# A one-core Hymba layer: the output stage's buffers moved, its mixing in place, the sample attention over another stage's memory, and other steps for the plan

## The chip, the cores and the metric

The kernel runs on one core of a Trainium2 chip. Its engines are TensorE (PE in the profile, with its weight loads as PEld), VectorE (DVE), ScalarE (ACT), GpSimd (POOL) and SyncE (SP, which here issues all the DMAs). Each engine takes its own instructions strictly in the order in which they stand; they wait for one another through semaphores. The metric is the time of one execution in microseconds of the device, as the median of the runs.

## The reference

One step of a one-layer hybrid decoder, on a prompt of 2048 tokens and a sample of 8 sequences with 8 tokens each, with model width 1024. Cut to what is computed:

```python
h = rmsnorm(x, norm_w)
q, k, v, qb, kb, vb, low, ga, gb = split(h @ w_in)          # one input projection
# mixer A: 8 heads x 64, q and k normed and rotated
branches = [dilated_attention(q, k, v, w, d) for w, d in ((128, 1), (512, 4), (2048, 16))]
oA = sum(softmax(lse of the branches)[g] * branches[g] for g in range(3))
# mixer B: gated linear attention (GLA), 4 heads, key 64, value 128
S[t] = exp(log_a[t]) * S[t-1] + kb[t] outer vb[t];  oB[t] = rmsnorm(qb[t] @ S[t])
y = x + concat(oA * silu(ga), oB * silu(gb)) @ w_out
```

The sample's queries see a cache of 2048 earlier keys and values for each sequence and an initial GLA state. Outputs are `y` for prompt and sample, the window of keys and values, the GLA states, and the sample's new keys and values.

## The kernel before, in words

**Tiles and stages.** The 2048 prompt tokens are 16 tiles of 128 rows; the sample's 64 rows are one more tile, called s. The stages overlap:

- Input stage. `prep` norms a tile of x, cuts it into two f16 parts and turns it with PE; `prep_first` does tiles s and 0 first, whose transposes are called th (early parts `early_ht`, result `hl`). `fetch_w` and `load_w` fetch the weight blocks v, k, q, qkb (GLA's q and k), g, vb, gb and at the end o0 and o1, the two halves of w_out. `fetch_w` reads a block, takes its maximum (mx_v on PE spreads it over the partitions), makes a scale `ns_v`, and cuts the block into an f16 high part on ACT (L1278) and a low part on DVE (L1279). `project` (L1728) multiplies a block with all 17 tiles, block after block, in accumulators acc_v, acc_k and so on (L1748). The tiles come back from DRAM as `hr`.
- Attention of the prompt (`unit`, `branch3`, `attend`): scores s, exponentials p, transposes t of p, products O with v. These are woven between the projections of q, qkb and g. The three branches are written to DRAM (`o_d`) with 66 numbers per head: 64 values, a denominator and a maximum.
- GLA (`gla_prompt`): chunks of 128 rows, worked in pairs e0 to e7. For a chunk there are scores (sc_e), a decay matrix `full` copied by ACT (L891), the product O with the old state `Sbd`, U (the new keys times the values, L1906), and four updates of the state on DVE (L1927). A norm follows (`gla_out`), and the chunk goes to DRAM as `ob_d`.
- Gates. `silu` (L1294) takes the accumulators of g and gb and writes ga and gw; `so_g` and `so_gb` are its tiles.
- Output stage. `scales` turns the maxima so far into the factors `smx` and `smxa` by which a tile's mixture is scaled into f16 range. `combine(t)` (L2124) loads the three branches of tile t as oc and GLA's result and the gates as ob, gw, ga, and mixes them into mix; `parts_of` (L2063) cuts mix into an f16 high and low part (mt); `turned` (L2070) transposes both (tm on PE, mh behind it); `finish` (L2097) does 48 matmuls Y (L2111) with w_out and adds x, which is loaded again as xr.
- Sample attention (`sample_pair`, `values`) for pairs of sequences: keys from the cache, scores, and products OS with the value tiles sv_b (four blocks of 512 columns, 1 MB) and sv_w (one block). It is woven between the Y of the output stage.

**What sets the order.** `weave` runs such generators in turn, and so writes the whole program down. Then the class `Plan` reads what was written: which instruction needs which, which tile lies in whose memory (a gate that opens only when the former holder is done), and a price for each instruction. `settle` works through the program backward and forward several times and so gives every instruction a priority; it then adds some hand-found numbers to the priorities of some of them, deals a last order, and `fix` ties every engine to it:

```python
prio = [-f for f in self.rank()]
for _ in range(rounds):
    self.order(prio, bias)
    prio = [-x for x in self.backward(self.start)]
...
plan.fix(plan.settle(7, 600.0, 1.15, 60.0, 10.0, steps))
```

`steps` was a list of seeds; `moved` (L637) drew from each which instruction is meant, how far the number reaches (its tile, itself, or neighbours in time on its engine), and the number. `land` (600) is added to the landing time of each DMA. So when one tile changes its memory, or one number changes, the order may change on all five engines, anywhere in the program.

**Memory.** Pools lie on the left or the right of each partition's memory. Pools of the input stage are wr (four slots for weight blocks), zp (two of each tag), hp (four, tag hl) and hps (one). They lie on the right and close at the end of the projection of gb. GLA's pools lie on the left. When GLA is done they close, and the output pools cb and cb1 take that memory: oc, mix, ob, gw, ga, mt, mh, xr and the small w, dw, mn, with two slots each, and three product tiles tc (tags t0 to t2) with one. The sample attention (sk2 and ss1) takes the input stage's memory on the right. `first_mixes` (L2197) mixes tiles 0 and 1 ahead of the output stage, beginning after gb's tile 11, and turns tile 0 after tile 14; it stands woven with the projection of gb and the loads of w_out.

## Time and profile before

| | |
|---|---|
| time, median of 3 runs | 1262.98 us (1262.38 to 1268.51) |
| the profiled execution | 1262.71 us, of which the profile's span is 1260.9 us |
| DVE, ACT, POOL busy | 956.1, 817.8, 549.0 us |
| mean traffic of the DMA queues | 225 GB/s, 283.08 MB |
| last projection (gb) ends | 1008.1 us after the span's start |
| output stage | 1008 to 1261 us |

The profile is one execution on the chip. A row of the list of waits gives the engine, the tile and line that waited, what released it, and then the total in us, the count and the longest. A row of the timeline gives the start, the duration, the engine, line, operation and tiles, the count of equal instructions that it stands for, and in brackets the idle time just ahead of it with its releaser. A row of grouped instructions gives `out<-in`, shape and count, then busy time and mean ns of one, then idle time ahead. The rows of slices divide the span by 40; a digit is the busy share in tenths, and PEclk is the granted clock of PE in tenths. The row by windows gives a stretch, its length, and then for each engine busy time and count, with the granted clock, the DMA share and GB/s at the end.

### The profile page before, as it was taken

The numbers are of one execution on the slowest core, as the hardware profiler recorded it, in microseconds if no ns is written. First come the engines' busy times: TensorE is split into PE (matmuls) and PEld (weight loads), VectorE is DVE, ScalarE is ACT, GpSimd is POOL, SyncE is SP. The second block draws the span as 40 slices with busy tenths as digits, with TensorE's granted clock in tenths as the row PEclk, the third lists the DMA queues.
The fourth block names the chain that finished last, engine by engine and source line by source line (L and its number), as shares of the span: only waits on it lengthen the run. The fifth ranks groups of instructions, "written<-read, shape, count | busy, mean of one in ns | idle before, by whom it ended". The sixth has DMA issues, their size and how long they took to land.

```text
span 1260.9 us, 26211 instructions
## 1 busy us (share of the span) xinstructions
PE 1202.4 (95%) x8942; PEld 723.7 (57%) x8942; DVE 956.1 (76%) x2450; ACT 817.8 (65%) x2191; POOL 549.0 (44%) x475
## 2 busy tenths in 40 slices
PE   5999999999999999998999999999999969999998
PEld 2444465667566566766677656665666435445443
DVE  7987887999889777777877557788888795269562
ACT  6654697889599888968778424678878632123220
POOL 0155433665755244643444766646533162024230
PEclk9999999999999999999999999999999979999999
DMA  8579935876945898699997867564435689988842
GB/s 291 187 213 270 258 126 138 233 200 188 231 153 148 232 251 301 183 272 273 265 272 231 242 184 195 172 209 137 139 135 193 217 299 343 381 333 326 323 169 68
DMA packets 235832, 283.08 MB, mean 225 GB/s; under 512 B 116193, under 2 KB 146866, under 8 KB 232626
## 3 DMA queue, kind: packets, MB, share of 16 engines
q1 hardware_dynamic: 235698, 281.40, 73.7%
q8 instruction: 71, 1.16, 0.4%
q14 instruction: 63, 0.52, 0.1%
HBM read 183.02 MB, written 75.24 MB: 205 GB/s over the span
## 4 chain that ended last, share of the span: by engine, by line
PE 53%; ACT 15%; DVE 15%; DMA 8%; issue 6%; SPq 2%; POOL 2%; DVEq 0%; ACTq 0%; POOLq 0%
PE Y L2111 13%; PE acc_v L1748 5%; PE acc_qkb L1748 4%; PE acc_k L1748 4%; PE acc_q L1748 3%; PE acc_vb L1748 3%; PE t L1046 3%; ACT p L1039 3%; PE O L1061 3%; PE s L1028 3%; PE acc_g L1748 3%; DMA o_d<-o 2%; PE OS L2360 2%; DMA qb<-q_d 2%; DVE p L1036 2%
## 5 line engine op out<-in xcount | busy, mean ns | idle before, releaser
L1748 PEld LDWEIGHTS <-hr 128*128 128x128 f16 x1824 | 172.0, 98 | 112.8 <-issue 13.2
L1603 POOL TENSOR_TENSOR pr<-k,qb 128x512 f32<-128x512 f32 x128 | 168.2, 1314 | 148.2 <-DVE sck L1604 73.9
L1039 ACT ACTIVATE p<-p,o 128x256 f32<-128x256 f32 (+1 forms) x384 | 173.7, 458 | 24.7 <-DVE o L1036 24.2
L1748 PEld LDWEIGHTS <-hl 128*128 128x128 f16 x1248 | 120.0, 98 | 119.5 <-issue 5.6
L2111 PE MATMUL Y<-w_o,mh 128*128 128x512 f16 x768 | 178.5, 383 | 2.4 <-ACT mh L2077 1.3
L1013 POOL TENSOR_TENSOR pt<-p,pt 128x512 f16<-128x512 f32 (+1 forms) x80 | 91.4, 1142 | 147.2 <-ACT pt L1012 124.1
L1061 PE MATMUL O<-v,pt 128*128 128x128 f16 x1200 | 135.6, 219 | 5.4 <-DVE pt L1009 1.9
L1046 PE MATMUL t<-ident,p 128*128 128x128 f32 x600 | 123.5, 278 | 4.7 <-ACT p L1039 3.0
L2111 PEld LDWEIGHTS <-mh 128*128 128x128 f16 x768 | 73.5, 99 | 89.5 <-issue 7.7
L1604 DVE TENSOR_REDUCE sck<-pr 128x8 f32<-128x512 f32 x128 | 86.9, 679 | 45.6 <-POOL pr L1603 45.2
L1061 PEld LDWEIGHTS <-pt 128*128 128x128 f16 x1200 | 93.7, 98 | 37.9 <-DVE pt L1009 4.6
L1748 PE MATMUL acc_g<-w_g,hr 128*128 128x256 f16 (+1 forms) x768 | 112.0, 276 | 0.0
L1748 PE MATMUL acc_v<-w_v,hl 128*128 128x512 f16 x384 | 108.5, 383 | 0.4 <-ACT zs_q L1323 0.4
L1748 PE MATMUL acc_k<-w_k,hl 128*128 128x512 f16 x384 | 104.4, 379 | 0.5 <-DVE vp L1410 0.4
L1748 PE MATMUL acc_vb<-w_vb,hr 128*128 128x512 f16 x384 | 100.9, 379 | 3.9 <-DVE so_g L1297 3.4
L1748 PE MATMUL acc_q<-w_q,hl 128*128 128x512 f16 x384 | 102.4, 379 | 0.1
L2159 POOL TENSOR_TENSOR tc<-oc,w 128x512 f32<-128x512 f32 x32 | 43.9, 1390 | 125.1 <-DVE w L2151 97.7
L1036 DVE CUSTOM_DVE_ANT_0 p<-s,m3w,scl_s 128x128 f32<-128x128 f32 (+1 forms) x256 | 87.7, 394 | 12.1 <-PE s L1028 4.7
L1748 PE MATMUL acc_gb<-w_gb,hr 128*128 128x512 f16 x384 | 94.8, 380 | 0.0
L1028 PE MATMUL s<-kk,qq 128*128 128x256 f16 (+1 forms) x512 | 87.7, 264 | 4.8 <-DVE o L1036 2.9
L1046 PEld LDWEIGHTS t<-ident,p 128*128 128x128 f32 x600 | 74.6, 141 | 26.8 <-ACT p L1039 11.5
L1748 PE MATMUL acc_qkb<-w_qkb,hr 128*128 128x512 f16 x288 | 81.0, 379 | 0.0
(528 smaller groups left out, 2532.4 us busy)
## 6 DMA issues: line engine op xcount, KB each, us to landing
k<-in_cache_k_win SPq DMA_DIRECT2D x104, 256.0 KB
sv_b<-in_cache_v_win SPq DMA_DIRECT2D x24, 1024.0 KB
hr<-h_d SPq DMA_DIRECT2D x44, 512.0 KB
qb<-q_d SPq DMA_DIRECT2D x64, 256.0 KB
oc<-o_d SPq DMA_DIRECT2D x48, 264.0 KB
o_d<-o SPq DMA_DIRECT2D x64, 132.0 KB
x<-in_x_prompt SPq DMA_DIRECT2D x16, 512.0 KB
h_d<-hl SPq DMA_DIRECT2D x16, 512.0 KB
```

The lines of the kernel that those rows point to most:

```text
L1013: POOL.tensor_tensor(l, f, h, ALU.subtract)
L1028: PE.matmul(s_ps[:, i * w : (i + 1) * w], q, k, start=(n == 0), stop=(n == len(prods) - 1),)
L1036: DVE.tensor_tensor_reduce(s[:, sl], s_ps[:, sl], mask, neg, BIG, ALU.add, ALU.min, nmf(i))
L1039: ACT.activation(s[:, sl], s[:, sl], AF.Exp, bias=nmf(i), scale=-1.0, accum_out=denf(i))
L1046: PE.transpose(p_ps[:, i * P : (i + 1) * P], t["s"][:, i * P : (i + 1) * P], ident[:])
L1061: PE.matmul(o_, t["pt"][:, c, (i * nb + b) * P : (i * nb + b + 1) * P], vf(i, b), start=(n == 0), stop=(n == 2 * nb - 1),)
L1603: POOL.tensor_tensor(pr[:], kt, qt, ALU.mult)
L1604: DVE.tensor_reduce(out, pr[:].rearrange("p (u k d) -> p u k d", u=2, k=4), AX.X, ALU.add)
L1748: PE.matmul(z, a_[:, k, :], w[:, p_, k, cols], start=(k == 0 and i == 0), stop=(k == KT - 1 and i == 2),)
L2111: PE.matmul(Y[:], a_[:, k, :], w_[:, part, k, :512], start=(i == 0), stop=(i == len(prods) - 1),)
L2159: eng.tensor_tensor(t_[:], oc[:, g, :, 0:64], w[:, g].unsqueeze(2).to_broadcast([P, NH, HD]), ALU.mult,)
L2360: PE.matmul(OS[32 * x : 32 * x + 32, 0:256], ps(x), vs_[bb][:, 256 * u : 256 * u + 256], start=(i == 0), stop=(i == 13),)
```

## The change

**Memory.** wr, zp, hp and hps now live to the end. A new pool `ca` lies beside them on the right while GLA's pools are still there; it holds oc, mix, ob, gw, ga, mn (two slots each) and the small tiles of `scales`. The tiles mt and mh take hp's four slots of tag hl, where the turned input tiles were; xr takes the four slots of wr. The sample attention's pools sk2 and ss1 lie on the left, over GLA's memory, after GLA closes; its small tiles vs_t, ls, k1, k1T, so and sv_w take slots of hps and zp.

**In place.** `combine` has no w, dw and tc any more: exponentials, denominators and the three products are written over oc, with a stride of 66 numbers per head.

**When.** `scales(0, 3)` is done after the gates of s, 0 and 1 and needs GLA's first two chunks only; the other 14 columns (`scales(3, 17)`) come after gb's tile 15. `first_mixes` mixes tiles 0 and 1 after gb's tiles 12 and 13 as written. The rest of GLA, the projection of gb, the loads of w_out and `first_mixes` are woven in one `weave`.

**Plan.** The steps now name kind, instruction and number directly (`some` for `moved`), there are other steps, and `settle` goes 12 rounds with a landing time of 900 ns more instead of 7 with 600. The number of matmuls is the same. Lines behind these edits move up by 6 to 24.

```diff
-        c_in, c_dot, c_first, c_att, c_b3 = (ExitStack() for _ in range(5))
+        c_dot, c_first, c_att, c_b3 = (ExitStack() for _ in range(4))
-        wr = right(c_in, "wr", 4)
-        zp = right(c_in, "zp", 2)
-        hp = right(c_in, "hp", 4)
-        hps = right(c_in, "hps", 1)
+        wr = right(c1, "wr", 4)
+        zp = right(c1, "zp", 2)
+        hp = right(c1, "hp", 4)
+        hps = right(c1, "hps", 1)
...
-        left = weave(host, gla_all, fetch, until=[gla_all])
-        c_gla.close()
-        cb = c1.enter_context(tc.tile_pool(name="cb", bufs=2, reuse_waits="tile"))
-        cb1 = c1.enter_context(tc.tile_pool(name="cb1", bufs=1, reuse_waits="tile"))
+        ca = right(c1, "ca", 2)
...
-            mt = cb.tile([P, 2, D], F16, name=f"mt_{tag}", tag="mt")
+            mt = hp.tile([P, 2, D], F16, name=f"mt_{tag}", tag="hl")
-            mhl = cb.tile([P, 2, KT, P], F16, name=f"mh_{tag}", tag="mh")
+            mhl = hp.tile([P, 2, KT, P], F16, name=f"mh_{tag}", tag="hl")
-            x = cb.tile([P, D], F32, name=f"xr_{tag}", tag="xr")
+            x = wr.tile([P, 2, 528], F32, name=f"xr_{tag}", tag="wr")
...
-            DVE.tensor_tensor(
-                w[:], nm, mn[:].unsqueeze(1).to_broadcast([P, 3, NH]), ALU.subtract
-            )
-            ACT.activation(w[:], w[:], AF.Exp, scale=-1.0)
-            DVE.tensor_tensor(dw[:], w[:], den, ALU.mult)
+            w = oc[:, :, :, 65]
+            DVE.tensor_tensor(w, w, mn[:].unsqueeze(1).to_broadcast([P, 3, NH]), ALU.subtract)
+            ACT.activation(w, w, AF.Exp, scale=-1.0)
+            DVE.tensor_tensor(den, w, den, ALU.mult)
...
+            o_ = [oc[:, g, :, 0:64] for g in range(3)]
             for g, eng in ((0, DVE), (1, POOL), (2, POOL)):
-                t_ = cb1.tile([P, NH, HD], F32, name=f"tc_{t}_{g}", tag=f"t{g}")
                 eng.tensor_tensor(
-                    t_[:], oc[:, g, :, 0:64],
-                    w[:, g].unsqueeze(2).to_broadcast([P, NH, HD]), ALU.mult,
+                    o_[g], o_[g], w[:, g].unsqueeze(2).to_broadcast([P, NH, HD]), ALU.mult
                 )
...
         def first_mixes():
+            while not {0, 1} <= mixed:
+                yield WAIT
+            scales(0, 3)
             for t in range(2):
-                while ("gb", 11 + t) not in done:
+                while ("gb", 12 + t) not in done:
                     yield WAIT
-                if t == 0:
-                    scales(0, 12)
...
+            while ("gb", NT - 1) not in done:
+                yield WAIT
+            scales(3, NT + 1)
...
-        weave(host, fetch, [first_mixes(), 2])
-        c_in.close()
-        scales(12, NT + 1)
+        mixed_first = [first_mixes(), 40]
+        weave(host, gla_all, fetch, mixed_first, until=[host, gla_all, fetch, mixed_first])
...
+        c_gla.close()
+        ssk = c1.enter_context(tc.tile_pool(name="sk2", bufs=2, reuse_waits="tile"))
+        ss1 = c1.enter_context(tc.tile_pool(name="ss1", bufs=1, reuse_waits="tile"))
...
-                    v = ssk.tile(
-                        [P, n, 512], F32, name=f"sv_{bp}_{bb}_{nm_}", tag=f"sv{n}",
-                        bufs=2 if n == 1 else 6,
+                    pool, tag, bufs = (zp, ("z3", "z4")[bb], 1) if n == 1 else (ssk, "sv4", 6)
+                    v = pool.tile(
+                        [P, n, 512], F32, name=f"sv_{bp}_{bb}_{nm_}", tag=tag, bufs=bufs
...
     steps = (
-        798993397, 379503271, 976436735, 990016090, 697217584, 129675417, 778155539, 369111627,
...
+        "1:9738:-1587 1:8521:-604 0:11378:-6896 2:12183:-36893 0:12042:-1940 0:7618:-507 "
...
-    plan.fix(plan.settle(7, 600.0, 1.15, 60.0, 10.0, steps))
+    steps = [tuple(int(v) for v in s.split(":")) for s in steps.split()]
+    plan.fix(plan.settle(12, 900.0, 1.15, 60.0, 10.0, steps))
```

Three places show how the order moved. The first is ACT at the start, before the first f16 part of w_v (L1278, afterwards L1272); jk is the square of an input tile, hl the copy of a turned one, hs the sample's. Before:

```order
L1104 ACTIVATE early_ht<-x_160,rs_189 128x1024
L1138 ACTIVATE hl_190<-th_0_266 128x1024
L1627 ACTIVATE nwa<-nw 128x8
L1101 ACTIVATE jk_225,ss_188<-x_160 128x1024
L1101 ACTIVATE jk_230,ss_188<-x_169 128x1024
L1164 ACTIVATE hs<-ptx_250 128x4x64
L1278 ACTIVATE w_v<-wr_v_154,ns_v 128x512
```

And after, on the same engine at the same place:

```order
L1098 ACTIVATE early_ht<-x_160,rs_189 128x1024
L1621 ACTIVATE nwa<-nw 128x8
L1095 ACTIVATE jk_225,ss_188<-x_160 128x1024
L1132 ACTIVATE hl_190<-th_0_266 128x1024
L1095 ACTIVATE jk_230,ss_188<-x_169 128x1024
L1158 ACTIVATE hs<-ptx_250 128x4x64
L1095 ACTIVATE jk_264,ss_188<-x_169 128x1024
L1272 ACTIVATE w_v<-wr_v_154,ns_v 128x512 x2
```

The copy hl stands behind one square, and a third square stands before the first part of w_v, where it stood behind it.

The second place is the end of the projection of gb. On DVE before, in the order in which the last silu product (L1305), the scales (L2052) and the mixing of tiles 0 and 1 stand:

```order
L2141 TENSOR_TENSOR mn_14036<-oc_14025 128x8
L2159 TENSOR_TENSOR tc_0_13953<-oc_13929,w_13941 128x512
L2142 TENSOR_TENSOR mn_14036<-mn_14036,oc_14025 128x8
L1297 TENSOR_SCALAR so_gb_14168<-acc_gb_14139,wi_gb 128x512
L2164 TENSOR_TENSOR tc_0_13953<-tc_0_13953,tc_1_13955 128x512
L2143 TENSOR_TENSOR w_14037<-oc_14025,mn_14036 128x24
L2155 SCALAR_TENSOR_TENSOR mix_14029<-obl_14030,smx,gwl_14032 128x512
L2147 TENSOR_TENSOR dw_14038<-w_14037,oc_14025 128x24
L1305 ISA so_gb_14168,gmax_b<-so_gb_14168,sa_gb_14170 128x512
```

And DVE after, from a copy of GLA's decayed keys (kdt_e of its last pair) on; the last silu product is L1299, the scales L2028 to L2034, a mixing step of tile 2 L2127, the state L1921, GLA's norm L907:

```order
L900 COPY kdt_e_13194<-ptk_e_13189 128x512
L1299 ISA so_gb_14169,gmax_b<-so_gb_14169,sa_gb_14171 128x512
L1299 ISA gmax_b 128x1
L2028 TENSOR_SCALAR bnd<-gmax_b,gm_n 128x14
L2029 TENSOR_TENSOR p_13340<-p_13340,bnd 128x14
L1184 TENSOR_SCALAR p_13340<-p_13340 128x14
L2031 RECIPROCAL smx<-p_13340 128x14
L2032 TENSOR_SCALAR smx<-smx 128x14
L2034 TENSOR_SCALAR smxa<-smx,pw_v 128x14
L2127 SCALAR_TENSOR_TENSOR mix_14228<-obl_14229,smx,gwl_14230 128x512
L1921 SCALAR_TENSOR_TENSOR Sbd_9605<-Sbd_9601,sums_e_13085,U_13198 64x128 x4
L907 TENSOR_REDUCE oss_c_13215<-osq_c_13214 128x4
```

Tiles 0 and 1 are mixed further up now, and the last pair of GLA stands behind the last silu. On PE the rows behind the last projection were the transposes of tile 0's low part and its first Y; here is PE after, from the last matmul of gb on:

```order
L1742 MATMUL acc_gb_14140<-w_gb,hr_13937 128x512
L1191 MATMUL mx_o_13922<-ident,w_o_13919 1x128
L853 MATMUL sc_e_64_13178<-qbd_9599,kq_e_13053 64x128 x4
L2052 LDWEIGHTS mt_14007
L2052 MATMUL tm_0_14120<-ident_83,mt_14007 128x128
L1194 MATMUL mx_o_13922<-mm_o_13924,one_row 128x1
```

The scores of GLA's last pair stand here, between the projection and the transposes tm_0; mx_o is the maximum of w_out's second half.

The third place is SP at the end of GLA, where it issues the value tiles of the cache. Before, ls_q and ls_k being the sample's new queries and keys:

```order
L2135 DMA gal_14405<-ga_d 128x512
L2257 DMA ls_q<-q_d 64x512
L2257 DMA ls_k<-k_d 64x512
L2391 DMA sv_0_b_14606<-in_cache_v_win 128x2048
L2391 DMA sv_1_b_14608<-in_cache_v_win 128x2048
L2391 DMA sv_0_w<-in_cache_v_win 128x512
```

And SP after, with the store of GLA's last chunk (L914), loads of x for the residual (xr) and masks of the sample attention (sm, mc, Sc) ahead of the first sv_b:

```order
L2077 DMA xr_14501<-in_x_prompt 128x1024
L914 DMA ob_d<-ob_c_13329 128x512
L2077 DMA xr_14675<-in_x_prompt 128x1024
L2105 DMA oc_14510<-o_d 128x528 x3
L2260 DMA Sc_14280<-sc_d 128x2x128
L2302 DMA sm_14475<-in_c_smask 128x448
L2304 DMA mc_14477<-in_c_smult 128x64
L2375 DMA sv_0_b_14574<-in_cache_v_win 128x2048
L2375 DMA sv_1_b_14576<-in_cache_v_win 128x2048
```

The sv_b stand behind a store that waits for GLA's last chunk, which they did not before.

132 lines of the change are left out of this document (72 added, 60 removed), and 32 rows, old and new, of the table steps.

## The prediction

> **What bounds the kernel now.** I read the page first, then the list of what TensorE (PE) waited for, then the timeline of PE where its idle time is thick, then VectorE (DVE) and ScalarE (ACT) at the same places.
>
> ```profile
> span 1260.9 us, 26211 instructions
> PE 1202.4 (95%) x8942; PEld 723.7 (57%) x8942; DVE 956.1 (76%) x2450; ACT 817.8 (65%) x2191; POOL 549.0 (44%) x475
> PE   5999999999999999998999999999999969999998
> PEclk9999999999999999999999999999999979999999
> ```
>
> PE is busy for 1202.4 of 1260.9 us: it is the bound, and no change of buffers removes a matmul. What can be won is its 58.5 us of idle time and the stretches at a low clock. The slices show two thick places: the first (tenths 5) and the 33rd (tenths 6, and the only slice with a clock below 9). The rest is spread thinly. The waits of PE, as total, times and longest:
>
> ```profile
> PE ptx L1159 <- DVE x_s L1149: 8.9, 1, 8.9
> PE tm L2076 <- ACT mt L2066: 8.8, 1, 8.8
> PE acc_vb L1748 <- DVE so_g L1297: 3.4, 4, 1.1
> PE t L1046 <- ACT p L1039: 3.0, 7, 1.1
> PE th L1132 <- ACT early_ht L1104: 3.0, 1, 3.0
> PE s L1028 <- DVE o L1036: 2.9, 6, 0.7
> PE O L1061 <- DVE pt L1009: 1.9, 3, 1.3
> ```
>
> Three groups: the start (ptx, th); the first tile of the output stage (tm waiting for mt); and many short waits inside the attention and projection stages: 3.4 + 3.0 + 2.9 + 1.9 = 11.2 us in the four largest rows. The second group, on PE's timeline:
>
> ```profile
> 993.66 14.42 PE L1748 MATMUL acc_gb<-w_gb,hr 128*128 128x512 f16 x66
> 1016.92 1.03 PE L2076 MATMUL tm<-ident,mt 128*128 128x128 f16 x8 [8.84 <-ACT mt L2066]
> 1019.07 0.61 PE L2111 MATMUL Y<-w_o,mh 128*128 128x512 f16 x1 [1.12 <-ACT mh L2077]
> ...
> 1020.33 5.70 PE L2111 MATMUL Y<-w_o,mh 128*128 128x512 f16 x15
> 1025.87 0.61 PE L2076 MATMUL tm<-ident,mt 128*128 128x128 f16 x8
> ...
> 1031.53 3.63 PE L2111 MATMUL Y<-w_o,mh 128*128 128x512 f16 x16
> ```
>
> After the last projection PE stands for 8.84 and 1.12 us, then works at a lower pace: 15 matmuls in 5.70 us (0.38 each) against 16 in 3.63 us (0.23 each) ten microseconds later. The mixed tile it waits for is late for a reason seen on DVE:
>
> ```profile
> 1001.45 0.17 DVE L2141 TENSOR_TENSOR mn<-oc 128x8 f32<-128x8 f32 x1
> ...
> 1013.38 1.78 DVE L1305 CUSTOM_DVE_ANT_0 so_gb<-so_gb,sa_gb 128x512 f32<-128x512 f32 x1
> ...
> 1017.38 2.06 DVE L2067 TENSOR_TENSOR mt<-mix,mt 128x1024 f16<-128x1024 f32 x1
> ```
>
> Combining tile 0 begins only at 1001.45, 6.6 us before the projections end, because its buffers lie where the linear attention (GLA) was; its 16 us of short DVE steps are laced with the last silus.
>
> **The transition: what is saved.** The waits 8.84 + 1.12 = 9.96 us. The low pace: 16 Y matmuls at 0.38 instead of 0.23 are 2.4 us, and eight transposes at 1.03 instead of 0.61, and a second group like it, are 0.84 us. Together 13.2 us. In the new order tiles 0 and 1 are mixed before the projection of tile 9 is evicted, their two f16 parts are cut before tile 13's silu ends, and the oc, ob, gw, ga loads of tiles 2 and 3 are issued ahead of the second half of w_out. So nothing of this wait should be left at tile 0.
>
> **The transition: what is put in its place.** The GLA's last pair of chunks, which ended beside the projections, now ends behind them, among the first transposes and Y matmuls. PE takes its instructions in order, so I follow the two chains that it will meet. The durations:
>
> ```profile
> 973.43 1.09 PE L859 MATMUL sc_e<-qbd,kq_e 128*64 128x128 f32 x8
> 977.15 0.43 PE L1906 MATMUL U<-vb,kdt_e 128*64 128x128 f32 x2
> 980.15 1.89 PE L1748 MATMUL acc_gb<-w_gb,hr 128*128 128x512 f16 x8
> 984.82 0.70 PE L1914 MATMUL O<-Sbd,kq_e 128*128 128x256 f32 x2 [0.57 <-ACT ob_c L919]
> 986.68 4.26 PE L1748 MATMUL acc_gb<-w_gb,hr 128*128 128x512 f16 x19
> 976.32 1.26 ACT L891 ACTIVATE full<-Ac_e 64x512 f32<-64x512 f32 x2
> 1010.68 0.63 ACT L1300 ACTIVATE sa_gb<-so_gb 128x512 f32<-128x512 f32 x1 [3.97 <-DVE so_gb L1297]
> 980.11 1.42 DVE L1927 SCALAR_TENSOR_TENSOR Sbd<-Sbd,sums_e,U 64x128 f32<-64x128 f32 x4
> L1279 DVE SCALAR_TENSOR_TENSOR w_o<-wr_o,ns_o,w_o 128x512 f16<-128x512 f32 x16 | 11.9, 766 | 0.8 <-ACT w_o L1278 0.8
> ```
>
> First chain: the projections of tiles 14 and 15 end together, so ACT has six silu steps (about 0.65 each, 3.9 us), three copies into `full` (0.63 each) and their waits for DVE, with tile 14 a microsecond ahead: about 5.7 us past the last projection. DVE then does the silu product (0.75, as a low part of w_o), the scales of 14 columns (six short steps of 0.17), a product of mix 2 (0.75) and only then the four state updates (1.42): about 9.6 us. Chunk 15's U takes a PSUM slot that those updates free. Until then PE has 0.6 us of scores, three groups of transposes (1.5), ptk (0.45), chunk 14's U and O (977.15 to 980.15, 3.0) and two Y with small transposes (0.7): 6.3 us. It waits 3.3 us, in pieces below 1 us.
>
> Second chain: w_out's second half. Its eight low parts (0.77 each, 6.1 us) follow on DVE after the state, the norm of chunk 14 and half of combining tile 2, and are laced with chunk 15's norm and tile 3: I add them up to about 23 us past the last projection. PE reaches the twelve matmuls that need the fourth part after U 15, 22 Y of the first half (4.9), chunk 15's O (984.82 to 986.68, 1.9) and the rest at about 19.7: it waits 3.5 us. Sum of what is put in place: 6.8 us. Low end 3 (DVE without the waits I gave it), high end 12 (the low pace comes back as well, 3.2, and DVE is later by 2).
>
> **The start.** PE's first rows and those that release them:
>
> ```profile
> 12.44 1.03 PE L1132 MATMUL th<-ident,early_ht 128*128 128x128 f16 x8 [3.00 <-ACT early_ht L1104]
> ...
> 16.40 0.37 PE L1197 MATMUL mx_v<-ident,w_v 128*1 128x128 f32 x1 [1.61 <-DVE w_v L1254]
> ...
> 19.44 0.58 PE L1444 MATMUL acc_v_s<-w_v,hs 128*128 128x512 f16 x1 [1.25 <-ACT w_v L1278]
> 15.40 0.68 DVE L1136 COPY hl<-th 128x1024 f16<-128x1024 f16 x1
> 15.57 1.04 ACT L1101 ACTIVATE jk<-x 128x1024 bf16<-128x1024 f32 x1
> 18.67 0.72 ACT L1278 ACTIVATE w_v<-wr_v,ns_v 128x512 f16<-128x512 f32 x1 [0.16 <-DVE ns_v L1269]
> ```
>
> Now the identity is loaded ninth instead of first, its f16 copy stands after the maximum of w_v on DVE, and so the 16 th transposes run after mx_v, not before. mx_v comes 1.0 us earlier (0.46 from the queue, 0.6 from the hl copy that is now behind it), at 15.4; the transposes (1.03 for eight) end at about 17.9, and the second mx_v step, which gives the scale, stands behind them, at 18.1. On ACT the copy of the transposed tile, a square (1.04), hs and a further square (1.04) now precede the first w_v, which starts at about 20.85 instead of 18.67. The slices behind the first show PE at 9, with nothing to swallow it, so I count the whole +2.1 us. Ends: 0 (the first slack swallows it) and +2.7.
>
> **The many short waits.** The rest of the order is dealt anew on every engine, with the same 8942 matmuls. The trace of before can't time it. Paces are read off the starts of neighbouring rows (O 0.50 us for nine, s 0.44 for four; a transpose of p took 0.11):
>
> ```profile
> 285.60 0.67 PE L1061 MATMUL O<-v,pt 128*128 128x128 f16 x9
> 286.10 0.60 PE L1028 MATMUL s<-kk,qq 128*128 128x256 f16 x4
> 286.54 0.38 PE L1748 MATMUL acc_q<-w_q,hl 128*128 128x512 f16 x1
> ```
>
> With these paces I counted how much other PE work the orders of before and after put between a step and the step that needs its eviction. From a unit's transposes to its O: under 1.5 us in 27 of 160 units before, 19 now. From the end of an accumulator to the next one in its slot: under 1 us in 11 of 168 before, 5 now. From scores to transposes: under 2 us in 5, now 3. Tight places fall from 43 to 27, by 37%; of 11.2 us that is 4.1 us. Ends: -8 (tight places decide nearly all) and +6 (half as much again; a new order makes its own late releases).
>
> **Edits that cost nothing, and their cover.** Combining in place writes the same 512 columns with a stride of 66 words; DVE is busy 76%, and in the list of waits PE was held by the mixing once, for the 8.8 us. mt and mh share four slots as they shared two and two. xr has four slots of wr instead of two: fewer waits on stores. vs_t, ls, k1 and sv_w take tiles of the input stage with as many slots as before. Without their cover each would cost its own 0.7 us at most per tile.
>
> **The sum**, against the profiled execution's own 1262.71 us (span 1260.9 and 1.8 around it; the median of the runs is 1262.98): 1262.7 - 13.2 + 6.8 + 2.1 - 4.1 = 1254.3, say 1254 us.
>
> **Rivals.**
> The waits move and don't shrink: the short waits stay as they are or grow by a few us, since 11.2 us in 20 places may be what any order leaves. Then 1262.7 - 13.2 + 6.8 + 2.1 + 0 to 3 = 1258 to 1261; I name 1260.
>
> The clock falls again. The row after the 8.84 us wait shows it: 0.38 per matmul, for about nine microseconds. In the new transition PE does transposes and short f32 work for nearly 10 us with waits between. Against it: waits of 1.1 us for so_g, in other slices, left PEclk at 9. Price 3.2 us: 1257.5. [...]
>
> Slower: the value loads of the cache become the bound. In SP's new order the first sv_b stands behind the store of chunk 15's output and ten short issues. Rows for the rate, the mean of the output stage, and for the present start:
>
> ```profile
> 1039.50:1197.00 157.50, 156.41 (x1269) 78.37 (x1267) 91.14 (x206) 40.54 (x65) 39.87 (x32) 1.00 0.91 343
> 1026.03 1.01 SPq L2391 DMA_DIRECT2D sv_b<-in_cache_v_win x2
> ```
>
> From O 15 to the first OS, PE has 58 Y and some transposes, 16 us, and 3.5 us of waits. I put the chunk's norm and store at 5 us and a landing at 2; ten issues at 0.5 take 5, two loads of 1 MB at 343 GB/s take 6.1: 18 us. The margin is 1.5 us. If it takes 6 us longer, each of the four pairs of rows stops PE by 4 to 5 us, 17 us in all: 1271. It decides from about 8 us per pair of loads. Against it: before, the first sv_b was issued at 1026.03 and no wait of PE for sv_b stands among the rows above.
>
> No gain at all: the chain of tile 0 is held by something the order doesn't show, and the transition stays: 1264. And much better: the tight places decide nearly all short waits and DVE is on time: 1262.7 - 13.2 + 4 + 1 - 8 = 1246.5.
>
> **How the numbers follow.** About 0.5% (6.3 us) is what a measurement of this kernel can tell from no change. Forecast (1250 to 1256) 0.40; much better 0.10; these are faster: 0.50. Waits that move 0.24, clock 0.08, no gain 0.05: within, 0.37. Loads late 0.13: slower. All low ends at once give 1262.7 - 13.2 + 3 - 8 = 1244.5, all high ends 1262.7 - 13.2 + 12 + 2.7 + 6 = 1270. From 1244 to 1268 the range leaves out most of the loads' case and the ends of others, some 0.15; the forecast's own range is 1250 to 1256.
>
> **What the profile after would show.** The wait of tm for mt (8.8 us) is gone, and no slice has PEclk below 9 behind the first. Between the last acc_gb and the second Y accumulator PE waits 5 to 8 us in pieces, for Sbd, `full`, and above all w_o. The first acc_v_s starts near 21.5. The waits of t, O, s and acc_vb in those four rows add up to about 7 us instead of 11.2. Wrong would be: w_o on time; th not after mx_v; OS waiting for sv_b for more than 3 us; or those four rows above 12 us.

## The result

The changed kernel takes 1268.6 us (median of 20 runs, 1262.33 to 1273.56), the kernel before 1264.64 us (20 runs, 1259.77 to 1268.51): a ratio of 1.0036, with a 95% interval of 1.0022 to 1.0049. It is slower by about 4.5 us; forecast were 1254 us with a range of 1244 to 1268, so it lies 14.6 us above the forecast and 0.6 us above the range, on the other side of no change. (The kernel before came to 1262.98 us in the three runs shown ahead of the prediction and to 1264.64 in the 20 here; the ratio is taken within the same rounds.) The profiled execution of the changed kernel took 1268.54 us, its span is 1266.8 us against 1260.9.

From the page of the changed kernel, the span, the busy time and PE's rows of the slices:

```profile
span 1266.8 us, 26198 instructions
PE 1200.7 (95%) x8942; PEld 725.5 (57%) x8942; DVE 956.7 (76%) x2450; ACT 816.5 (64%) x2191; POOL 553.5 (44%) x475
PE   4999999999999899998999999999999979999998
PEclk9999999999999999999999999999999999999999
```

PE does the same 8942 matmuls and is busy 1.7 us less (1200.7 for 1202.4), but the span is 5.9 us longer: PE idles 66.1 us instead of 58.5. The slice of the transition has gone from 6 to 7, and no slice has a clock below 9. One more slice of PE in the first half has fallen to 8. The list of PE's waits after:

```profile
PE mx_v L1191 <- DVE w_v L1248: 14.9, 1, 14.9
PE s L1022 <- DVE o L1030: 4.9, 7, 1.7
PE s L1022 <- DMA kk<-kp_d: 4.8, 3, 3.3
PE Y L2088 <- DVE w_o L1273: 4.1, 2, 2.1
PE O L1055 <- DVE pt L1003: 2.5, 3, 1.8
PE acc_k L1742 <- DVE vp L1404: 2.5, 2, 1.7
PE O L1055 <- POOL pt L1007: 2.4, 3, 1.1
PE U L1900 <- DVE Sbd L1921: 2.3, 2, 1.9
PE t L1040 <- DMA hr<-h_d: 1.9, 1, 1.9
PE acc_vb L1742 <- DVE so_g L1291: 1.6, 3, 0.9
...
PE t L1040 <- ACT p L1033: 1.2, 1, 1.2
```

The wait of tm for mt (8.8 us) is gone. In its place stand w_o (4.1), Sbd (2.3) and some smaller ones. New in the attention are kk (1.8 us before, 4.8 now), the accumulator of k waiting for vp (0.4, now 2.5), O waiting for the low part that POOL makes (1.1, now 2.4) and a late reload hr (not there before).

By stretches, PE alone, first before and then after (length, busy time and count, clock, DMA share, GB/s):

```profile
20.00:200.00 180.00, 173.46 (x1024) 1.00 0.73 208
200.00:562.00 362.00, 355.45 (x2686) 1.00 0.78 213
...
837.10:1256.30 419.20, 402.78 (x3023) 0.98 0.67 238
```

```profile
20.00:200.00 180.00, 172.25 (x996) 0.99 0.71 203
200.00:562.00 362.00, 349.02 (x2655) 1.00 0.77 209
...
843.30:1262.40 419.10, 404.24 (x3101) 1.00 0.67 238
```

The idle time grows most between 200 and 562 us, in the attention: 13.0 us for 6.6. The list of waits of that stretch alone has these two at its top, where before has 0.3 and 0.7:

```profile
PE s L1022 <- DMA kk<-kp_d: 4.1, 2, 3.3
PE s L1022 <- DVE o L1030: 3.5, 5, 1.7
```

The last row of each of the two tables above runs from half a microsecond ahead of the first matmul of the projection of gb to the last Y, so it holds the transition and the whole output stage: 419.2 us before and 419.1 after. The equal length doesn't mean that nothing was won there, because the work in it is not the same. After holds 78 matmuls more in it, nearly all of them GLA's that came earlier before; its PE idles 14.9 us there for 16.4, and its clock is 1.00 for 0.98. The stretch that these matmuls left, from the first matmul of the projection of g to the first of gb, is 2.6 us shorter after:

```profile
561.09:837.63 276.54, 266.59 (x2194) 1.00 0.82 225
```

```profile
569.85:843.80 273.95, 263.96 (x2122) 0.99 0.86 227
```

Ahead of these stretches both have done the same work, to within a matmul. So in these two executions the changed kernel is 8.8 us late at the first matmul of g and wins back 2.9 us behind it: the loss lies ahead of the transition, and the transition, of which the prediction expected 6.4 us, gave a part of that.

The start and the transition on PE's timeline after:

```profile
14.95 0.37 PE L1191 MATMUL mx_v<-ident,w_v 128*1 128x128 f32 x1 [14.95 <-DVE w_v L1248]
...
15.55 1.89 PE L1126 MATMUL th<-ident,early_ht 128*128 128x128 f16 x16
...
20.87 0.59 PE L1438 MATMUL acc_v_s<-w_v,hs 128*128 128x512 f16 x1 [1.79 <-ACT w_v L1272]
...
1021.07 0.66 PE L1900 MATMUL U<-vb,kdt_e 128*64 128x128 f32 x8 [1.87 <-DVE Sbd L1921]
...
1031.37 2.28 PE L2088 MATMUL Y<-w_o,mh 128*128 128x512 f16 x9 [1.99 <-DVE w_o L1273]
1035.72 1.45 PE L2088 MATMUL Y<-w_o,mh 128*128 128x512 f16 x6 [2.07 <-DVE w_o L1273]
1038.32 0.61 PE L2052 MATMUL tm<-ident,mt 128*128 128x128 f16 x8 [1.15 <-ACT mh L2053]
...
1042.12 0.88 PE L2293 MATMUL tk<-ident,k 128*128 128x128 f32 x6 [1.25 <-DVE qx L2256]
```

The order at the start came out as forecast (th behind mx_v), with the first acc_v_s at 20.87 us where 21.5 was said. The waits for Sbd, w_o, mh and qx in the transition are 8.3 us in these rows.

### The profile page after: what moved, and what is told of

Same layout as the page of the kernel before. It is cut to its first block, busy times and chain, and to the rows that moved or that the text cites. A ratio compares the mean times of both kernels' runs of the same rounds, so it can differ in the third digit from the quotient of the medians.

```text
span 1266.8 us, 26198 instructions
## 1 busy us (share of the span) xinstructions
PE 1200.7 (95%) x8942; PEld 725.5 (57%) x8942; DVE 956.7 (76%) x2450; ACT 816.5 (64%) x2191; POOL 553.5 (44%) x475
## 5 line engine op out<-in xcount | busy, mean ns | idle before, releaser
L1033 ACT ACTIVATE p<-p,o 128x256 f32<-128x256 f32 (+1 forms) x384 | 173.1, 456 | 31.5 <-DVE o L1030 29.0
L1055 PE MATMUL O<-v,pt 128*128 128x128 f16 x1200 | 131.4, 220 | 8.9 <-DVE pt L1003 2.5
L1040 PE MATMUL t<-ident,p 128*128 128x128 f32 x600 | 118.8, 279 | 3.3 <-DMA hr<-h_d 1.9
L1742 PE MATMUL acc_q<-w_q,hl 128*128 128x512 f16 x384 | 106.4, 383 | 1.1 <-ACT zs_k L1317 0.8
L1742 PE MATMUL acc_g<-w_g,hr 128*128 128x272 f16 (+1 forms) x768 | 105.9, 278 | 0.0
L1742 PE MATMUL acc_vb<-w_vb,hr 128*128 128x512 f16 x384 | 97.6, 383 | 1.7 <-DVE so_g L1291 1.6
L1040 PEld LDWEIGHTS t<-ident,p 128*128 128x128 f32 x600 | 75.0, 142 | 21.5 <-ACT p L1033 8.7
L2130 POOL TENSOR_TENSOR oc<-oc 128x512 f32<-128x512 f32 x32 | 42.4, 1343 | 100.8 <-DVE oc L2123 58.7
```

Source lines behind the costliest of these rows:

```text
L1033: ACT.activation(s[:, sl], s[:, sl], AF.Exp, bias=nmf(i), scale=-1.0, accum_out=denf(i))
L1040: PE.transpose(p_ps[:, i * P : (i + 1) * P], t["s"][:, i * P : (i + 1) * P], ident[:])
L1055: PE.matmul(o_, t["pt"][:, c, (i * nb + b) * P : (i * nb + b + 1) * P], vf(i, b), start=(n == 0), stop=(n == 2 * nb - 1),)
L1742: PE.matmul(z, a_[:, k, :], w[:, p_, k, cols], start=(k == 0 and i == 0), stop=(k == KT - 1 and i == 2),)
L2130: eng.tensor_tensor(o_[g], o_[g], w[:, g].unsqueeze(2).to_broadcast([P, NH, HD]), ALU.mult)
```

## The experiments

Each ratio is to the kernel before on the same chip in the same rounds. "Order" always means the order of the instructions on all five engines.

| kernel | median, us | ratio to before (95%) |
|---|---|---|
| early_before | 1304.43 | 1.0352 (1.0321 to 1.0384) |
| early_after | 1325.61 | 1.0511 (1.0483 to 1.0538) |
| layout_only | 1282.45 | 1.0166 (1.0140 to 1.0192) |
| plan_only | 1317.99 | one run |
| fill_before | 1261.13 | 0.9993 (0.9980 to 1.0007) |
| first_before | 1259.16 | 0.9975 (0.9962 to 0.9987) |
| first_after | 1267.22 | 1.0039 (1.0026 to 1.0052) |
| no_low | 1264.84 | 1.0024 (1.0008 to 1.0041) |
| before_no_steps | 1284.64 | 1.0177 (1.0142 to 1.0211) |
| after_no_steps | 1285.46 | 1.0183 (1.0153 to 1.0213) |
| half_before | 1258.61 | 0.9975 (0.9962 to 0.9987) |
| searched | 1271.30 | 1.0078 (1.0061 to 1.0096) |
| start_before | 1264.57 | 1.0027 (1.0011 to 1.0042) |
| hundred_before | 1261.55 | 0.9998 (0.9984 to 1.0013) |

### Is it the order or the layout: two orders joined, first badly, then well

The first 10586 of the 13290 instructions are the same in both programs. So one kernel's order can be given to the other's first part. The kernel's plan is told the place of each instruction instead of working it out:

```diff
-    plan.fix(plan.settle(12, 900.0, 1.15, 60.0, 10.0, steps))
+    place = [...]   # one number for each instruction
+    plan.fix({
+        e: sorted((n for n in range(plan.real) if plan.eng[n] == e), key=place.__getitem__)
+        for e in plan.ENGINES
+    })
```

The first two kernels are divided by the place in the written program.

> The changed kernel, but with the first 10586 instructions as written (all up to the projection of gb; they are the same instructions in both kernels) in the order that they had before, on every engine; everything behind in the order of after. Theory A: the change loses in the order of this early part (in the two profiled executions PE idles 9.3 us longer there, and the granted clock falls four times for 3.41 us) and wins about 5.8 us behind it, by the transition and the clock there. Then this kernel takes 1264.6 - 5.8, about 1259 us (1256 to 1261), with no fall of the clock at 8.8 us of wait. Rival B: the layout costs (mixing in place with a stride of 66 words, pools held to the end), whatever the early order is: then about 1268, like after.

> The kernel before, but with the same first 10586 instructions in the order that they have after; everything behind in the order of before. Theory A: it keeps the 8.8 us wait and its fall of the clock, and adds the losses of the early part: 1268.6 + 5.8, about 1274 us (1271 to 1277). Rival B: the early order is worth nothing, 1264 to 1266 us.

Both came out far slower than either parent (1.0352 and 1.0511), as neither theory had it. The seam was in the wrong place: GLA's instructions are written before the projection of gb but run beside it, so from that projection on two orders were laced together. The largest wait of PE in early_after:

```profile
PE tm L2098 <- ACT mt L2088: 30.9, 1, 30.9
```

It is the mixing's, as those that grew in early_before are GLA's (u_e for gT_e, 4.8 us at the longest). These two say nothing on the layout. The next pair is divided by time, at the first matmul of the projection of g (562 us), where nothing of the two orders is laced.

> The changed kernel with the order of before up to the first matmul of the projection of g (6241 instructions, 562 us: start, projections of v, k, q, qkb and most of the attention), and its own order from there; the seam lies between two projections, so that GLA, which runs later, is dealt by one order alone. Theory A (the order of the attention part is what the change loses): the kernel takes 2 to 6 us less than before. Rival B (the layout costs): 3 to 5 us more than before, like after.

> The kernel before with the order of after for the same 6241 instructions, and its own order from there. Theory A: 5 to 11 us more than before, by idle time and falls of the clock ahead of 570 us, with the 8.8 us wait of the transition as it was. Rival B: as before, within 2 us.

The changed kernel with the old order in its first 562 us is faster than before (0.9975, -3.2 us), and the kernel before with the new order there is slower (1.0039, +4.9 us). Theory A holds, with the second just below the 5 to 11 us that it said; rival B, in which the layout costs, falls: what the change does behind 562 us, layout and order together, is worth a gain of about 0.25%, and the loss is the new order of the first 562 us. Almost all that runs there are instructions that both programs have alike. The two don't quite add: -3.2 and +4.9 make +1.7, where after shows +4.5, with intervals of about 1.6 us on each. PE between 200 and 562 us, first_before and then first_after:

```profile
200.00:562.00 362.00, 355.05 (x2683) 1.00 0.78 213
```

```profile
200.00:562.00 362.00, 351.07 (x2670) 1.00 0.77 212
```

The idle time goes with the order: 6.6 us before and 7.0 in first_before, 13.0 after and 10.9 in first_after, and so do the two waits: in these 362 us s waits for kk 1.0 us in first_before and 2.8 in first_after, and for o 0.7 and 3.3 us.

### Where in the first 562 us

> The changed kernel with the order of before up to the first matmul of the projection of qkb only (4437 instructions, 414 us), and its own order from there. If the loss lies in the waits that the traces with the order of after all show (products O waiting for the low part of pt at 182 to 205 us, scores waiting for kk near 350 us): 1 to 5 us less than before, like the kernel with before's order up to 562 us. If it lies in the second half of the attention: 2 to 5 us more than before.

> The changed kernel with the order of before in its first 28 us only (identity first, th ahead of mx_v, the first part of w_v with fewer squares ahead of it), and its own order from there. If the prediction's term for the start is right as it stands (+2.1 us, counted whole), this takes about 2 us less than after, so about 2.5 us more than before. If the start is swallowed by later waits: as after, 4 to 5 us more than before.

> The changed kernel with the order of before in its first 100 us, and its own order from there. If the loss sits in the waits between 180 and 360 us that the order there brings with it (O for the low part of pt, scores for kk): those waits stay, and it takes 3 to 5 us more than before, like after. If it sits in what the first 100 us leave behind (which tiles and DMAs are how far when the attention begins): the waits at 180 to 205 us shrink, and it takes 2 to 4 us less than before.

The ratios of the changed kernel with the old order up to 0, 28, 100, 414 and 562 us are 1.0036, 1.0027, 0.9998, 0.9975 and 0.9975. So the first 28 us cost about 1.1 us, the stretch from 28 to 100 us 3.7, that from 100 to 414 us 2.9, and from there to 562 us nothing; each of these carries some 2 us of uncertainty, the first is not clear of zero. half_before came out as its first branch said. start_before, 3.4 us above before, lies between its two. hundred_before lies between its two: the time is like before's, but the waits stay. Here are PE's largest waits between 170 and 260 us in the kernel after:

```profile
PE O L1055 <- POOL pt L1007: 2.4, 3, 1.1
PE O L1055 <- DVE pt L1003: 1.8, 1, 1.8
PE acc_k L1742 <- DVE vp L1404: 0.8, 1, 0.8
```

The same list of hundred_before has these very rows, to the tenth of a microsecond, although 100 us of another order run ahead of them: the order carried these waits with it. Between 28 and 100 us the loss is not one wait. From 20 to 100 us PE idles 2.2 us after and 0.1 us both before and in hundred_before, of which the waits shown make 1.0 (acc_q for zs_k 0.76 and for w_q 0.26); behind it acc_k waits for vp at 122 us, 1.67 us after and 0.63 in hundred_before. That makes some 3 of the 3.7 us.

### The parts of the change by themselves

layout_only has the new tiles, mixing and weaving with the old `settle(7, 600.0, ...)`, `moved` and seeds; plan_only the reverse. The two without steps differ from their parents in one line each:

```diff
-    steps = (
-        798993397, 379503271, ...
+    steps = ()
...
-        "1:9738:-1587 1:8521:-604 ...
+    steps = ""
```

> The changed kernel's tiles, in-place mixing and weaving, with the plan of before (its seeds, 7 rounds, 600 ns). A third order of all engines comes out. Theory A (orders decide, the layout is worth a few us): between 1260 and 1272 us, and where it stands is told by idle time of PE and falls of the clock ahead of 837 us, not by the output stage, whose time from the third tile on stays within 2 us of that of after. Rival B (the layout costs): above 1268, with the loss in the output stage.

> The kernel before with the plan of after (its steps, 12 rounds, 900 ns). The steps name instructions by their place in the written program, which is another from instruction 10586 on, so behind it they hit others. Theory A (the numbers belong to one program): clearly slower, 1275 to 1320 us, most of it as idle time of PE. Rival C (the new numbers are a better plan by themselves): 1255 to 1264 us.

> The kernel before with an empty list of steps: priorities from the backward passes alone. Theory A (the order is what is tuned, and the layout's worth is small against it): about 15 to 30 us more than before. Rival: within 5 us of before.

> The changed kernel with an empty list of steps (12 rounds and 900 ns as it has). Theory A: 20 to 40 us more than before, and at or above the kernel before without steps; then the layout and the new settings alone win nothing, and the new steps make up for it less well than the old ones did. Rival G (the layout is better by itself): 5 us or more below the kernel before without steps.

layout_only is slower than both kernels (1.0166), outside what theory A allowed and above the 1268 us that rival B named. But its loss is not in the output stage, where rival B put it. In its trace the projection of g begins at 571.5 us (561.1 before), from there to the end of gb's projection it takes 456.5 us (447.0 before), and from there to the last Y 247.8 us (248.2 before). Among its largest waits behind the start are those in the attention and one of the sample attention:

```profile
PE s L1028 <- DVE o L1036: 6.5, 12, 1.9
PE R L2276 <- POOL Scg L2271: 6.1, 1, 6.1
```

plan_only, of which there is one run, is slower by 57 us, as theory A had it, 19 of them in one wait:

```profile
PE tm L2070 <- ACT mt L2060: 18.8, 1, 18.8
```

Without steps the two kernels are level (1.0177 and 1.0183): the layout and the new settings alone win nothing that two runs can show, and hand-found steps are worth some 22 us in the kernel before and 18 in the one after. That is the size against which a change of 4 us stands. Each list of numbers serves only the program for which it was found.

### Does the clock fall cost time

Both parents run at half the pace in places. At the start the matmuls acc_v stand 0.43 us apart up to 24.90 us before and 24.00 us after, and 0.22 us from there on. Behind the 8.8 us wait before the granted clock is 0.50 for 13.65 us, and after it is 0.50 in four stretches of 3.41 us. fill_before keeps PE at work with matmuls whose result nobody reads.

```diff
+        def warm(name, w, x, groups):
+            t = ps_Y.tile([P, 512], F32, name=name, tag="Y")
+            for n in groups:
+                for _ in range(n):
+                    PE.matmul(t[:], w, x, start=True, stop=True)
+        wt = ptp.tile([P, 2, 512], F16, name="warm_w", tag="pt")
+        DVE.memset(wt[:, 0], 0.0)
+        warm("warm_0", wt[:, 0, :P], wt[:, 0], (20, 10, 6, 5))
...
+                if tag == "0" and nh == 0:
+                    many = ident16[:].unsqueeze(1).to_broadcast([P, 4, P])
+                    warm("warm_1", ident16[:], many, (38, 6))
```

> The kernel before, every engine in its old order, with 85 matmuls added on PE that compute nothing that is used (f16, 128x512, into an accumulator slot that is free): 41 in the idle time of the start (20 ahead of ptx, 10 ahead of th, 6 ahead of mx_v, 5 ahead of acc_v_s) and 44 in the wait of the transition (38 ahead of tm, 6 ahead of the first Y). Theory C: the granted clock goes by how much PE does in a stretch of 3.41 us, so the half rate at the start (19.4 to 24.9 us, 2.7 us lost) and behind the 8.8 us wait (3.5 us lost) both go, and the kernel takes 6 us less than before. Rival D: the clock goes by something else (time since the start, what other engines do); then the added work changes nothing, or costs up to 2 us where it runs into the work behind it.

Both half rates went, as theory C said, but the time did not follow. PE's timeline in the transition of fill_before, and its stretch by windows:

```profile
1003.71 2.75 PE L1759 MATMUL acc_gb<-w_gb,hr 128*128 128x512 f16 x12
...
1023.98 0.62 PE L2087 MATMUL tm<-ident,mt 128*128 128x128 f16 x8 [1.56 <-ACT mt L2077]
...
1035.39 9.01 PE L2125 MATMUL Y<-w_o,mh 128*128 128x512 f16 x41
```

```profile
1006.50:1045.30 38.80, 34.83 (x212) 1.00 0.85 314
```

and the row of the kernel before that answers to the last but one:

```profile
1036.98 9.01 PE L2111 MATMUL Y<-w_o,mh 128*128 128x512 f16 x41
```

The transposes take 0.62 us for eight instead of 1.03, the clock is 1.00 throughout. Yet from the end of the projection to the run of 41 Y it is 28.9 us in both (1006.46 to 1035.39, and 1008.08 to 1036.98): where PE had crawled, it now waits 1.56 us for mt of tile 1, and in smaller pieces for mh. In the kernel before, the half rate behind the long wait cost nothing, as tile 1 was not ready any sooner. At the start it is alike: the first acc_v_s starts 1.1 us earlier, at 18.37, the next acc_v 0.22 us behind it, and in this trace nothing of that is left by the first matmul of the second projection of v (acc_vb_s), at 569.0 us before and 569.1 here. The warm matmuls show the pace coming up: PE is busy with eight of them in the 3.25 us from the first at 1.19 us on (0.41 each), and with thirteen in the 2.83 us from 4.44 us on (0.22 each), so in this trace the full pace came 3.25 us after the first.

After's own falls, by windows of PE (the stretch ahead of a fall, then the fall):

```profile
184.41:187.82 3.41, 2.37 (x17) 1.00 0.52 185
187.82:191.24 3.42, 2.89 (x17) 0.50 0.40 96
```

Three more are at 352, 580 and 686 us. Each lasts 3.41 us at a clock of 0.50 and would cost half of that, 1.7 us, if PE alone set the pace (an estimate). Over the 20 runs of after, time and mean clock go together (1260.6 us of span at a clock of 0.997, 1271.5 at 0.992, a correlation of -0.86), but the waits ahead of a fall lengthen a run as well, so what a fall costs in the attention is not shown.

### What bounds the transition now

no_low takes DVE's work for the second half of w_out away; that half is then multiplied with its high f16 part alone.

```diff
             for k in range(KT):
                 h, l = w[:, 0, k, :n], w[:, 1, k, :n]
                 ACT.activation(h, raws[k], AF.Copy, scale=nws[:, k : k + 1])
+                if name == "o1":
+                    POOL.memset(l, 0.0)
+                    yield
+                    continue
                 last_low[0] = DVE.scalar_tensor_tensor(
```

> The changed kernel in its own order, but the second half of w_out is left with its f16 high part: its eight low parts on DVE (L1273, 0.74 to 1.8 us each in the transition) are replaced by eight memsets of zeros on POOL, put ahead of the transition at about 985 us. Theory E (the transition is bound by DVE: from 1016 to 1046 us it has no idle time, and PE waits there for Sbd, w_o, mt and qx, all DVE's): the 4.1 us for w_o go, and those for mt and qx shrink; 3 to 8 us less than after, so 1 to 4 us less than before. Rival F (the waits are those for the weights' load and ACT's high part, or move to the next step): less than 2 us from after's time, 3 to 5 us more than before.

1.0024 against after's 1.0036, which is 1.5 us and no more than the two intervals allow by chance: rival F. The 4.1 us for w_o are gone from its trace, and this stands in their place, on PE, ACT and DVE:

```profile
1032.82 1.01 PE L2056 MATMUL tm<-ident,mt 128*128 128x128 f16 x8 [3.82 <-ACT mh L2057]
...
1030.80 1.06 ACT L2046 ACTIVATE mt<-mix 128x1024 f16<-128x1024 f32 x1 [1.91 <-DVE mix L2139]
1031.76 1.01 ACT L2057 ACTIVATE mh<-tm 128x1024 f16<-128x1024 f16 x1
...
1030.07 0.69 DVE L2139 TENSOR_TENSOR mix<-oc,gal 128x512 f32<-128x512 f32 x1 [1.16 <-POOL oc L2138]
```

The copy mh that PE needs stands on ACT behind the f16 part of the next tile, which waits for that tile's mixing on DVE, which in turn waited 1.16 us for POOL's sum. Theory E, which expected 3 to 8 us, falls: with DVE's eight low parts gone, a chain of short steps on three engines sets the end of the transition, with the mixing of tile 2 as its last part, which the weights covered in the kernel after. One thing is left open: in this trace PE runs at half the pace from 1017.41 us (four Y in 1.87 us) and again from 1032.82 us, behind the wait for mh (eight transposes in 1.01 us), while after has 0.61 us for eight transposes there and a clock of 1.00. What these two took from the gain is not shown.

### Another order on the new layout

searched has a table of places as above, found by some 10000 trial moves on the plan's own prices with landings of 600 ns.

> The changed kernel's tiles and instructions, with an order found by some 10000 more trial moves on the plan's own prices at a landing time of 600 ns. Theory A (the layout is no loss, another order on it can beat both kernels): 3 to 10 us less than before. Rival H (an order fitted that closely to the plan's prices is fragile: by the same prices with landings 300 ns later it takes 18 us more): 0 to 10 us more than before, by waits of PE for DMAs (kk, hr, k, qq).

1.0078: slower than both, inside the 0 to 10 us that rival H named, but not by the cause that it named, since PE's list of waits has none for a DMA. Why this order is slow stays open. A wait of the mixing is among those that grew (1.1 us after):

```profile
PE tm L2052 <- ACT mh L2053: 5.5, 5, 2.2
```

half_before and first_before are the versions that beat both kernels, by 3.2 us (0.13 to 0.38%) against before.

## Why the prediction was wrong, step by step

**The many short waits** are the step that failed, with its sign: -4.1 us were forecast, and a loss was measured. With the start in it, it is about +7.7 us on the changed kernel (from 1.0036 with the new order to 0.9975 with the old one up to 562 us, 0.61% of 1264.6) and +4.9 us on the kernel before (first_after), each with some 2 us of uncertainty; with start_before's 1.1 us taken off, 6.6 and 3.8. (What the new order does to the short waits behind 562 us was not separated from the rest.) Three things in its working were wrong. It took one threshold of 1.5 us for the way from a unit's transposes to its O, but there are two ways. Half the units go over ACT and DVE, half over two ACT copies and POOL, and the step on POOL took longer than the one on DVE (medians of 1161 and 685 ns). The profile's view of the tile pt after has a row for each (count, then shortest, median and longest in ns, and the stretch):

```profile
L1007 POOL TENSOR_TENSOR pt<-p,pt x80: 670/1161/2001, 156.5 to 715.0; 128x512 f16<-128x512 f32 x70, 128x256 f16<-128x256 f32 x10
L1003 DVE SCALAR_TENSOR_TENSOR pt<-t,pt x80: 404/685/692, 156.7 to 714.4; 128x512 f16<-128x512 f32 x70, 128x256 f16<-128x256 f32 x10
```

With the k-th first copy on ACT paired with the k-th low part, the traces of before and after give medians of 1.65 us from the start of the copy to the end of the low part by DVE and 3.0 us by POOL. So places counted as safe were not: O for POOL's part went from 1.1 to 2.4. No place was counted between a reload such as kk, a DMA, and the scores that need it, the row that grew most. Then it counted places and not lengths, though a few long waits make most of the sum. And it looked only at the four rows that were largest before. Those came to 10.2 us after, which is neither the 7 forecast nor above the 12 that was to be the sign of an error; the growth is in one of the four, s for o (2.9 to 4.9), and in rows that were small before: kk 1.8 to 4.8, acc_k 0.4 to 2.5, hr 0 to 1.9, O for POOL 1.1 to 2.4. None of the four signs of being wrong that the prediction named came, for they looked where it had counted. Of the two measured sizes one lies 0.6 us above the end of +6 that was given for this term and one inside it, so the sign is shown to be wrong and that end is not.

**The transition: what is saved** held, as far as the traces show. The waits of 9.96 us did go, and so did the low pace, 3.24 us of the sum: from 1010 to 1050 us after has the full clock. fill_before is no objection. It takes the low pace away in the kernel before and wins nothing, as tile 1 is late there; in the changed kernel all waits of tm for mt come to 0.6 us. In the kernel before the slow stretch cost nothing, 28.9 us with it and without it, because what came behind it was late; that it would have cost its 3.24 us in the changed kernel is the author's estimate.

**The transition: what is put in its place** was right in kind and mis-sized, 6.8 us where PE now idles 10.1. Chunk 15's U waited 1.9 us for Sbd (3.3 forecast) and w_o 4.1 us (3.5 forecast). Not foreseen were tm for mh and mt (1.7), tk for qx (1.3) and smaller ones; all idle time from 1010 to 1050 us is 10.1 us, inside the ends of 3 to 12. (The prediction's two figures for the second chain, 23 and 19.7 us, give 3.3 us, not the 3.5 that it added.) Thus 13.2 saved and 10.1 put in place leave 3.1 us, where 6.4 were forecast. first_before, with the old order in front, is faster than before by 3.2 us; that the two agree so closely may be chance, since its 3.2 us hold all that the change does behind 562 us. no_low shows that another chain stood directly behind.

**The start** was right in its mechanism (20.87 us, 21.5 forecast; ends 0 to 2.7) and too large in its worth: the prediction counted the whole 2.1 us because no slice showed slack to swallow it. start_before puts it at 1.1 us, not clear of zero. The first acc_v_s is late by 1.4 us in the trace (20.87 for 19.44), and part of that PE has caught up by 25 us, since its matmuls reach their full pace (0.38) at 24.90 us before and at 24.00 after.

**The edits that cost nothing** weren't tried one by one. With the old order in front the changed kernel is 3.2 us faster, so the stride of 66 words and the shared slots do not cost more than the rest of the change wins behind 562 us. In first_before's trace the gain lies between the first matmul of g and the first of gb (272.6 us for 276.5), which GLA's matmuls left; from there to the end it takes 2.2 us more than before, with 75 matmuls more and one fall of the clock. What the layout is worth without its new order was not measured.

**The rivals.** The value loads (slower by 17 us) didn't come: no wait of OS for sv_b is in the list, though the order on SP is as described. The nearest was the one in which the waits move and don't shrink, which allowed them to grow by 3 us; they grew by more. The rival of no gain has its 1264 us near the 1268.6 measured, but not its cause, for the wait of tile 0 is gone; the prediction gives no sum for it. The clock fell again, but not where that rival had it. It fell in the attention and the projections, behind waits of 0.2 to 3.3 us, and the prediction's inference from waits of 1.1 us, that short ones do no harm, was wrong. Its evidence, a digit 9 of PEclk, can't show such a fall: 3.41 us at half rate in a slice of 31.5 us still leave 0.95. Ahead of the fall at 188 us PE was busy 2.37 of 3.41 us, and no gap was above 0.71. In the transition after, the clock stayed up:

```profile
1010.00:1050.00 40.00, 29.89 (x234) 1.00 0.69 231
```

In first_before it fell there for one stretch, behind the wait for Sbd, in the same work with nearly the same waits:

```profile
1008.91:1012.32 3.41, 1.35 (x17) 1.00 0.26 73
1012.32:1015.73 3.41, 3.41 (x16) 0.50 0.86 278
```

So the rival was not what happened, but it lay close, and whether the transposes and the short f32 work that it named bring the clock down is not settled here.

## What to carry to other kernels

When an edit makes a planner deal every engine's order anew, the new order is the change, and the edit may be a detail of it: measure the edit under an order held fixed wherever the program is the same, as first_before does, before believing either. A count of tight places foretells nothing if the ways between two steps differ in length; take each way's own duration from the trace, and look at the longest few. And a slow clock need not cost time: in fill_before the full rate in place of the half left the 28.9 us of the transition as they were, because the work behind was not ready; fill it and see.

## What was not expected of the hardware

- A fixed order repeated its waits to a hundredth or two of a microsecond (1.11, 0.42, 0.72, 0.21, 0.53 and 1.79 us in hundred_before; 1.12, 0.42, 0.71, 0.21, 0.53 and 1.79 after, 4 us later), while whole runs of one kernel spread by 0.9% (after, 1262.33 to 1273.56 us).
- The falls of the clock to one half lasted 3.41 us each at 187.82, 351.66, 580.36 and 686.17 us after, and four times that, 13.65 us, behind the 8.8 us wait before. fill_before had the full pace at 4.44 us, before at 24.90 and after at 24.00.
- PE's busy time in the stretch ahead did not tell by itself whether the clock fell: it fell behind 2.37 us of 3.41 (products of 128 columns and f32 transposes) and did not behind 1.45 us (Y, 512 columns):

```profile
1034.33:1037.74 3.41, 1.45 (x6) 1.00 0.92 239
```

Leaving out the products with the identity parts these two (1.3 us of the first stretch are left, all 1.45 of the second), but not others of the same trace. In the stretch from 1037.74 us only 0.97 us are left and the clock stayed, in that from 348.25 us 1.09 us and it fell. What is counted stays open.
